# Moving top-k rounds, rotation copies, mask tiles and stores in a one-core encoder block

## The chip, the cores and the metric

The kernel runs on one core of one Trainium2 chip. The core has engines with queues of their own: PE (TensorE) multiplies matrices, DVE (VectorE) and ACT (ScalarE) work on tiles element by element, POOL (GpSimd) and SP (SyncE) here mostly issue DMAs. Each engine runs its instructions strictly in the order in which the program gives them. The metric is the device time of one execution in microseconds (us).

## What is computed

One layer of an encoder block on 512 frames of 2048 channels. A combined projection feeds a sparse attention (an index score picks 128 keys for each frame), a retention mixer with rotary positions, and two merge gates; then come output projections and a gated embedding. Cut to what matters here:

```python
h = rmsnorm(x, norm_gain)
proj = h @ w_in                       # split into 13 parts
# sparse attention, by chunks of 64 frames, topk = 128
index = einsum(relu(einsum(qi, ki)), w)
index = where(admissible, index, -inf)
_, sel = lax.top_k(index, topk)
bias = rel_table[t5_bucket(pos_sel - pos)]
logits = q @ k[sel] * scale + bias
a_out = softmax(logits) @ v[sel] * silu(az)
# retention, 8 heads
rq, rk = rope(rq, positions), rope(rk, positions) * R_KEY_DIM ** -0.5
scores = (rq @ rk) * intra_decay
y = scores @ rv + (rq * from_start) @ state
b_out = groupnorm(y) * silu(rz)
merged = sigmoid(ga) * (a_out @ w_a_out) + sigmoid(gb) * (b_out @ w_b_out)
r = x + merged @ w_o
out = rmsnorm(r + (p @ w_ple) * sigmoid(r @ w_ple_gate), final_gain)
```

## The kernel before

Everything is computed transposed: channels on the 128 partitions, 512 frames along the free dimension. Float32 weights are multiplied as two float16 parts. ACT rounds a tile of 128x1024 weights to its high part (`wh`, line 228), and DVE subtracts this from the weights to get the low part (`wl`, line 133). Both stand in rings of three tiles, so neither engine can run far ahead of PE. Units of weights are split three ahead (`AHEAD`) and loaded eight ahead.

Most of the projection is done in pairs of output blocks by `gemm_pair`, a seven-product scheme in 14 runs of 8 matmuls (112 matmuls). The products gather in the banks `ps_p`, `ps_v`, `ps_q`, `ps_r`. Four copies by ACT (`pv`, `e1`, `e2`, `e3`, line 341) and additions by DVE (`e_t`, line 345, and `go`, line 1212) make the two output blocks. A table, `SPLIT_AT`, says before which run which unit is split. DMAs that accumulate into a weight tile (line 193, POOL) and one addition by DVE (line 239) make the sums of weights that the scheme needs.

The order on each engine is written by hand. `step()` is called after every two matmuls of a pair (after three elsewhere) and counts ticks. `later(n, f)` runs `f` n ticks on. When nothing else is queued in `todo`, `step` takes one entry of the background queue `bg` every `state["rate"]` ticks. Behind the index scores, `bg` holds, in this order: sums of the normalized input, the top-k rounds, and the masks of the position bias.

A top-k round takes the eight largest entries of each row of a 128-row tile (`MAX8`) and then overwrites them (`MATCH_VALUE_LOAD` and `MATCH_REPLACE8`). There are 16 rounds for each of three tiles of 256, 384 and 512 columns, 48 in all. The last round of a tile writes the mask `mneg`, which attention adds to the bias. A mask of the bias is an ACT `Sign` over a row of positions (line 902). Four banks of masks at a time go through PE (`bias_mm`) and ACT to the DRAM tensor `scr`, from which attention loads its bias.

The stages in order of time: index queries and scores; the retention's values (`values`, twice) and the attention's values (`values_pair`); eight heads, each with one pair for the retention's query and key and two pairs for the merge gates; four pairs for `rz`, eight for the attention's queries and keys, four for `az`; attention beside `project_b`; the output projections; the embedding gate; the end.

At the end of a retention pair, `rotate` takes each of the two output blocks: two ACT copies that swap its halves (`rb`, lines 1012 and 1013), then two products and a sum on DVE (lines 1014 to 1016). The query scaling (`qt`, line 1023), the scores (`ps_rs`), the decay (`at`), the transposed keys (`kn`) and the states follow at fixed ticks, in the list `steps`.

ACT also issues DMAs: evicted values (`rd`), gates (`sgb`, `sga`, line 1222). Small tiles come from a pool of 28 general slots (`U`), larger ones from five big slots (`B`).

Of the kernel before, what the change touches and what calls it, by code (L numbers as in the profile page):

```python
# [17 lines left out]
OP = mybir.AluOpType  # L18
# [50 lines left out]
def block_kernel(tc, flag, cfg, xT, pT, posb, posq, w_in, w_v, w_r0, w_r1, w_ik, w_a, w_b, w_o, w_ple, w_gate,  # L69
# [7 lines left out]
    with contextlib.ExitStack() as ctx:  # L77
# [11 lines left out]
        def U(name, dt=F32):  # L89
            return up.tile([128, L], dt, name=name, tag="u")  # L90
# [226 lines left out]

        def gemm(ids, parts, name, c=ALL, order=None):
            return gemms([(ids, slice(0, 128), parts, c, name)], order=order)[0]

# [611 lines left out]

        rounds = [lambda r=r, t=t: topk_round(t, r == 15) for r in range(16) for t in range(1, NT)]
        bg.append(lambda: xn_load(0))
# [3 lines left out]
        bg.extend(rounds)  # L938
        bg.append(lambda: state.update(rate=BG_RATES[3]))
        banks = [(t, tuple(range(8 * t + g, 8 * t + g + n))) for t, n in reversed(tuple(enumerate((4, 2, 1, 1))))  # L940
                 for g in range(0, 8, n)]
        for n in range(0, len(banks), 4):
            run = banks[n:n + 4]
            bg.extend([lambda b=b, i=i, j=j: bias_mask(b, i, j > 1) for j, b in enumerate(run)
                       for i in range(4 * len(b[1]))])
            bg.append(lambda run=run: waiting.append(run))

        def split(src, name, lag=0, gain=None, checked=True):
# [49 lines left out]
        def retention(h):  # L998
# [10 lines left out]
            def rotate(i, o):  # L1009
                E[i] = o  # L1010
                b = U("rb")
                act.activation(b[0:64, :], o[64:128, :], AF.Copy)
                act.activation(b[64:128, :], o[0:64, :], AF.Copy)
                later(3, lambda: dve.tensor_mul(o, o, ct))
                later(5, lambda: dve.tensor_mul(b, b, st))
                later(7, lambda: dve.tensor_add(o, o, b))
                if i:
                    for n, f in steps:
                        later(n, f)
# [79 lines left out]

            steps = [(9, queries), (24, scores), (24, lambda: keys(0)), (28, decay), (29, lambda: keys(1))]  # L1100
            steps += [(n, lambda i=i: states(i)) for i, n in enumerate((39, 41, 43))]
            steps += [(51, lambda t=t: values_out(t)) for t in range(NT)]
# [12 lines left out]
        for i in range(2):  # L1115
            for t, ps in enumerate(values(u_rv[i], RV[i], x_load if i else lambda s: None)):
                later(3 * t, lambda i=i, t=t, ps=ps: act.dma_start(rd[i, t, :, 0:RV[i]], normal(ps, t, RV[i])))
        state["rate"] = BG_RATES[1]
# [83 lines left out]
        def hold(on):  # L1202
            state["hold"] = on

        def gate_pair(ids, finish):
            t = B("go")
            outs = [t[:, 0:512], t[:, 512:1024]]
            have = [0, 0]

            def done(c0, c1, i, q):  # L1210
                o = outs[i]
                dve.tensor_add(o[:, q], c0, c1)  # L1212
                have[i] += 1
                if have[i] == 2:
                    later(1, lambda: finish(i, o))

            gemm_pair(ids, Xh, done)

        def to(dst, func):
            def finish(i, o):  # L1220
                act.activation(o, o, func, scale=un_x)  # L1221
                act.dma_start(dst[i], o)
            return finish

        for h in range(NH):
            if state["rate"] == BG_RATES[2]:
                later(38, lambda: hold(True))
                later(64, lambda: hold(False))
            gate_pair(u_r[h], retention(h))
            for n in (2 * h, 2 * h + 1):  # L1230
                d, m = ((sgb, 2 * n), (sga, 2 * n - 16))[n >= 8]
                gate_pair(u_g[n], to(d[m:m + 2], AF.Sigmoid))
# [179 lines left out]
        for n in range(NH // 2):  # L1412
            if n == NH // 2 - 1:
                while bg or waiting:
                    bg.popleft()() if bg else bias_banks(waiting.popleft())
                for h in range(NH):
                    later(4 + 3 * h, lambda h=h: b_load(h))
                heads = [attention_head(h) for h in range(NH)]
                later(38, heads[0].pop(0)[1])
            gate_pair(u_az[n], to(zd[2 * n:2 * n + 2], AF.Silu))  # L1420
# [10 lines left out]
        for h in range(NH):  # L1431
            for n, f in heads[h]:
                later(max(n + HEAD * h + 10, 0), f)

# [110 lines left out]
        def finish_pair(n, s):  # L1545
# [30 lines left out]
            for i, f in zip(at, (mul, own, add, squares, lambda: gains(0), lambda: gains(1), sums)):  # L1576
                later(i, f)

        for m in range(ME):
            if m % 2 == 0:  # L1580
                later(8, lambda m=m: pw_load(m))
                s = B("go")
            pg = gemm(u_e[m], rparts, "ps_pg", order=R_ORDER if m == 0 else None)
            act.activation(half(s, m % 2), pg, AF.Sigmoid, scale=un_r)
            if m % 2:
                finish_pair(m // 2, s)
# [219 lines left out]
BG_RATE = 4  # L1806
BG_RATES = (2, 5, 40, 7, 5)
ADD_LAG = 24
X_BACK = (4, 6, 8, 10, 12, 14, 22, 24, 26, 28, 30, 32)
HEAD = 13  # L1810
WARM = 11
MANUAL = True
QK_LOW = 5, 9

# [102 lines left out]
```

## Time and profile before

| | |
|---|---|
| median of 3 runs | 1575.38 us (1575.31 to 1577.98) |
| profiled execution | 1577.83 us, of which the span is 1576.0 us |
| DVE, ACT, POOL busy | 83%, 60%, 14% of the span |
| mean granted clock of PE | 0.996 |

The page gives the busy time of each engine. The view of waits lists who waited for whom, with the total, the number and the longest in us. The table by stage cuts the time at given points. The timeline lists instructions in order of time, with the idle time before each and what ended it in brackets. A matmul's end is modelled, so neighbouring matmuls overlap in it and a short stop of PE may not show as idle time.

### The profile page before, as it was taken

Reading aid. Unit: us, or ns where it says so; the run is one execution under the profiler, and the core shown is the slowest. Engines: PE = TensorE matmul, PEld = TensorE weight load, DVE = VectorE, ACT = ScalarE, POOL = GpSimd, SP = SyncE. Lnnn points to the kernel's source line nnn. Section 1 sums busy time; section 2 is a strip of 40 time slices with the busy share of each in tenths; the row PEclk is TensorE's granted clock in tenths of the full one; section 3 lists DMA queues with packets and bytes.
Section 4 is the critical chain, followed back from the end, with each engine's and each line's share of the span. In section 5 each row is a group of like instructions: output and inputs, shape, how many; then the busy total and the mean of one; then the engine's idle time right before and its main releaser. Section 6 shows DMA issues by size and latency. Waiting matters only on the chain.

```text
span 1576.0 us, 25637 instructions
## 1 busy us (share of the span) xinstructions
PE 1549.7 (98%) x9321; PEld 893.4 (57%) x9321; DVE 1312.7 (83%) x2699; ACT 950.1 (60%) x1475; POOL 225.2 (14%) x254
## 2 busy tenths in 40 slices
PE   9999999999999999999999999999999999999996
PEld 5654445666665655566565566555544556545764
DVE  8899889989988988987777877786668888888875
ACT  7566545555555555676877776566644455576653
POOL 3100111111111111112332122100000111100101
PEclk9999999999999999999999999999999999999998
DMA  8436889789788889789999899998566799876973
GB/s 318 131 118 207 254 205 253 199 216 240 194 214 222 199 205 234 179 224 256 251 278 245 222 248 237 257 366 307 177 212 193 199 224 240 220 228 188 256 243 111
DMA packets 127882, 353.40 MB, mean 224 GB/s; under 512 B 15360, under 2 KB 28160, under 8 KB 127744
## 3 DMA queue, kind: packets, MB, share of 16 engines
q1 hardware_dynamic: 87280, 228.63, 42.9%
q0 software_dynamic: 27360, 98.06, 33.7%
q10 hardware_dynamic: 13104, 24.96, 4.3%
q8 instruction: 75, 1.23, 0.3%
q14 instruction: 63, 0.52, 0.1%
HBM read 308.60 MB, written 42.99 MB: 223 GB/s over the span
## 4 chain that ended last, share of the span: by engine, by line
PE 43%; DVE 4%; ACT 3%; issue 1%; ACTq 0%; DVEq 0%
PE ps_p L402 13%; PE ps_v L402 9%; PE ps_q L402 4%; PE ps_r L402 4%; PE ps_w L309 2%; PE ps_w L310 2%; PE ps_w L308 2%; DVE wl L133 1%; ACT bm L1319 1%; PE ps_pg L1667 1%; PE ps_pg L1669 1%; PE ps_pg L1668 1%; PE ps_pg L310 1%; ACT bm L1326 1%; DVE rl L133 1%
## 5 line engine op out<-in xcount | busy, mean ns | idle before, releaser
L133 DVE SCALAR_TENSOR_TENSOR wl<-wraw,wh 128x1024 f16<-128x1024 f32 (+3 forms) x472 | 565.0, 1208 | 123.2 <-ACT wh L228 120.0
L228 ACT ACTIVATE wh<-wraw 128x1024 f16<-128x1024 f32 (+3 forms) x471 | 483.8, 1038 | 225.3 <-DVE wraw L239 114.4
L402 PEld LDWEIGHTS <-wh 128*128 128x128 f16 x3008 | 293.6, 98 | 311.2 <-ACT wh L228 9.7
L402 PEld LDWEIGHTS <-wl 128*128 128x128 f16 x2912 | 283.3, 98 | 74.0 <-DVE wl L133 9.5
L193 POOL DMA_DIRECT2D wraw<-w_in x120 | 106.5, 966 | 545.5 <-DVE wl L133 342.6
L402 PE MATMUL ps_p<-hs,wh 128*128 128x512 f16 x640 | 151.2, 379 | 0.0
L341 ACT ACTIVATE e<-ps_p 128x512 f32<-128x512 f32 x152 | 89.8, 591 | 62.3 <-PE ps_p L402 57.0
L402 PE MATMUL ps_p<-hs,wl 128*128 128x256 f16 x640 | 83.1, 273 | 3.6 <-DVE wl L133 2.7
L402 PE MATMUL ps_r<-hs,wh 128*128 128x512 f16 x320 | 77.3, 385 | 5.9 <-ACT wh L228 5.9
L402 PE MATMUL ps_q<-ha,wh 128*128 128x512 f16 x320 | 75.7, 379 | 0.0
L402 PE MATMUL ps_p<-ha,wh 128*128 128x512 f16 x320 | 75.6, 379 | 0.0
L402 PE MATMUL ps_v<-hs,wh 128*128 128x512 f16 x320 | 75.6, 379 | 0.0
L402 PE MATMUL ps_v<-ha,wh 128*128 128x512 f16 x320 | 75.6, 379 | 0.0
L310 PEld LDWEIGHTS <-wl 128*128 128x128 f16 x460 | 45.0, 98 | 49.9 <-DVE wl L133 2.3
L1212 DVE TENSOR_TENSOR go<-e_t 128x256 f32<-128x256 f32 x160 | 68.2, 426 | 5.8
L308 PEld LDWEIGHTS <-wh 128*128 128x128 f16 x460 | 45.1, 98 | 44.3 <-ACT wh L228 0.5
L309 PEld LDWEIGHTS <-wh 128*128 128x128 f16 x460 | 45.0, 98 | 44.0
L193 POOL DMA_DIRECT2D wraw<-w_o x24 | 21.1, 941 | 327.8 <-DMA sm<-mbs 181.7
L902 ACT ACTIVATE mk<-relf,thr 128x512 f16<-128x512 f32 (+3 forms) x128 | 66.5, 554 | 1.6 <-ACT go L1221 1.6
L239 DVE TENSOR_TENSOR wraw<-wraw 128x1024 f32<-128x1024 f32 x52 | 63.7, 1225 | 1.8
L1221 ACT ACTIVATE go<-go 128x512 f32<-128x512 f32 x40 | 25.2, 631 | 64.3 <-DVE go L1212 64.3
L345 DVE TENSOR_TENSOR e_t<-ps_p,pv 128x512 f32<-128x512 f32 x48 | 33.1, 690 | 24.8 <-ACT e L341 24.7
(421 smaller groups left out, 2870.9 us busy)
## 6 DMA issues: line engine op xcount, KB each, us to landing
wraw<-w_in SPq DMA_DIRECT2D x170, 512.0 KB, 5.2
wraw<-w_in POOLq DMA_DIRECT2D x120, 512.0 KB, 8.0
wraw<-w_o SPq DMA_DIRECT2D x32, 512.0 KB, 5.5
wraw<-w_o POOLq DMA_DIRECT2D x24, 512.0 KB, 7.6
wraw<-w_gate SPq DMA_DIRECT2D x24, 512.0 KB, 5.2
wraw<-w_v SPq DMA_DIRECT2D x16, 512.0 KB, 6.8
wraw<-w_b SPq DMA_DIRECT2D x16, 512.0 KB, 6.2
wraw<-w_a SPq DMA_DIRECT2D x16, 512.0 KB, 4.1
```

The costliest lines, as they stand in the source:

```text
L133: dve.scalar_tensor_tensor(l, src, 1.0 if gain is None else gain, h, op0=OP.mult, op1=OP.subtract, **({"accum_out": column()} if checked a ...
L193: pool.dma_start(out=view(raw_tiles[r], nk, cols), in_=src[:, k0:k0 + nk, :], accum_op=OP.add)
L228: act.activation(h, raw, AF.Copy, scale=cfg.w)
L239: dve.tensor_add(raw, raw, view(raw_tiles[plus], nk, cols))
L308: pe.matmul(o, h[:, k, w], a, start=(s == order[0]), stop=False)
L309: pe.matmul(o, h[:, k, w], b, start=False, stop=False)
L310: pe.matmul(o, l[:, k, w], a, start=False, stop=(s == order[-1]))
L341: act.activation(E[n], src, AF.Copy)
L345: f(t, x, y)
L402: pe.matmul(o[:, co], w[:, k], src, start=(n < 4 and begin and k == 0 and j == 0), stop=(ended[n] == 16), skip_group_check=True)
L902: act.activation(bias_e[b][i // per][:, ln * (i % per):ln * (i % per + 1)], relf[:, :ln], AF.Sign, bias=thr[:, q:q + 1])
L1212: dve.tensor_add(o[:, q], c0, c1)
```

## The change

It applies to the kernel's fast variant, the one that runs here.

- Top-k: rounds that are left when the heads begin leave the background queue and are cut in two, `largest` (MAX8) and `remove` (the rest). In each head a half runs at ticks 15 and 44 and two at tick 106; in each pair behind the heads one at ticks 19 and 44. What is then left runs ahead of the last `az` pair. Masks start in the last head.
- `rotate`: for the second block the copies, products and sum come 8, 9, 11 and 13 ticks after the block is done, not 0, 3, 5 and 7. Scores, keys, decay and states follow four (states three) ticks later.
- Masks: all of them take general slots; two of four banks took big slots. Behind the heads one comes every sixth tick, not every fifth.
- Stores of values and gates by ACT are issued two ticks after the instruction that makes them.
- The splits of the first wide value weights, and of the second unit of the first embedding-gate weight, are asked for earlier.
- Attention heads start two ticks earlier.

```diff
+        def topk_halves(r, t):
+            a = R["isc"][:, IOFF[t]:IOFF[t] + 128 * (t + 1)]
+            m8 = []
+            def largest():
+                m8.append(S("m8", 8))
+                dve.max(m8[0], a)
+            def remove():
+                dve.match_replace(out=a, in_to_replace=m8[0], in_values=a, imm_value=-3.39e38)
+                if r == 15:
+                    dve.tensor_scalar(mneg[:, TOFF[t]:TOFF[t] + 128 * (t + 1)], a, -3.3e38, NEG,
+                                      op0=OP.is_gt, op1=OP.mult)
+            return largest, remove
...
+        n_behind = [-len(bg)]
+        if not fast:
+            bg.append(lambda: state.update(rate=BG_RATES[3]))
...
-            bg.extend([lambda b=b, i=i, j=j: bias_mask(b, i, j > 1) for j, b in enumerate(run)
+            bg.extend([lambda b=b, i=i, j=j: bias_mask(b, i, j > 1 and not fast) for j, b in enumerate(run)
...
+        n_behind[0] += len(bg)
...
             def rotate(i, o):
                 E[i] = o
-                b = U("rb")
-                act.activation(b[0:64, :], o[64:128, :], AF.Copy)
-                act.activation(b[64:128, :], o[0:64, :], AF.Copy)
-                later(3, lambda: dve.tensor_mul(o, o, ct))
-                later(5, lambda: dve.tensor_mul(b, b, st))
-                later(7, lambda: dve.tensor_add(o, o, b))
+                def swap():
+                    b = E["b"] = U("rb")
+                    act.activation(b[0:64, :], o[64:128, :], AF.Copy)
+                    act.activation(b[64:128, :], o[0:64, :], AF.Copy)
+                at = ROTATE_AT[i] if fast else ROTATE_AT[0]
+                later(at[0], swap)
+                later(at[1], lambda: dve.tensor_mul(o, o, ct))
+                later(at[2], lambda b=E: dve.tensor_mul(b["b"], b["b"], st))
+                later(at[3], lambda b=E: dve.tensor_add(o, o, b["b"]))
...
-            steps = [(9, queries), (24, scores), (24, lambda: keys(0)), (28, decay), (29, lambda: keys(1))]
-            steps += [(n, lambda i=i: states(i)) for i, n in enumerate((39, 41, 43))]
+            steps = [(9, queries), (28, scores), (28, lambda: keys(0)), (32, decay), (33, lambda: keys(1))]
+            steps += [(n, lambda i=i: states(i)) for i, n in enumerate((42, 44, 46))]
...
         for i in range(2):
-            for t, ps in enumerate(values(u_rv[i], RV[i], x_load if i else lambda s: None)):
-                later(3 * t, lambda i=i, t=t, ps=ps: act.dma_start(rd[i, t, :, 0:RV[i]], normal(ps, t, RV[i])))
+            def each(s, i=i):
+                if i:
+                    x_load(s)
+                    if fast and s == KT - 2:
+                        split_to(u_av[0][0] + AHEAD)
+            for t, ps in enumerate(values(u_rv[i], RV[i], each)):
+                def values_away(i=i, t=t, ps=ps):
+                    v = normal(ps, t, RV[i])
+                    later(2 if fast else 0, lambda: act.dma_start(rd[i, t, :, 0:RV[i]], v))
+                later(3 * t, values_away)
...
+        late_rounds = collections.deque()
+        def late_round():
+            if late_rounds:
+                late_rounds.popleft()()
         def gate_pair(ids, finish):
+            if state["banks"]:
+                for n in ROUNDS_AT:
+                    later(n, late_round)
...
                 act.activation(o, o, func, scale=un_x)
-                act.dma_start(dst[i], o)
+                later(2 if fast else 0, lambda: act.dma_start(dst[i], o))
...
+        if fast:
+            while len(bg) > n_behind[0]:
+                late_rounds.extend(halves[bg.popleft()])
+            state["rate"] = 1 << 30
         for h in range(NH):
+            if fast and h == NH - 1:
+                state["rate"] = BG_RATES[3]
...
+            if fast:
+                for n in ROUNDS_IN_HEAD:
+                    later(n, late_round)
...
+                todo.extend([late_round] * len(late_rounds))
...
-                later(max(n + HEAD * h + 10, 0), f)
+                later(max(n + HEAD * h + (8 if fast else 10), 0), f)
...
+        def split_second(s):
+            if s == 14:
+                split_to(u_e[0][1] + AHEAD)
...
-            pg = gemm(u_e[m], rparts, "ps_pg", order=R_ORDER if m == 0 else None)
+            pg = gemm(u_e[m], rparts, "ps_pg", order=R_ORDER if m == 0 else None,
+                      each=split_second if fast and m == 0 else None)
...
-BG_RATES = (2, 5, 40, 7, 5)
+BG_RATES = (2, 5, 40, 7, 6)
+ROTATE_AT = (0, 3, 5, 7), (8, 9, 11, 13)
+ROUNDS_AT = 19, 44
+ROUNDS_IN_HEAD = 15, 44, 106, 106
```

What it does to the order on the engines is shown at three places. First ACT where the retention pair of the sixth head ends and the next pair begins: `rb` are the copies of the rotation, `e` and `pv` copies of products, `wh` roundings. Before:

```order
L1012 ACTIVATE rb<-go 64x512
L1013 ACTIVATE rb<-go 64x512
L341 ACTIVATE e_6030<-ps_p 128x512
L228 ACTIVATE wh<-wraw 128x1024
L1012 ACTIVATE rb<-go 64x512
L1013 ACTIVATE rb<-go 64x512
L228 ACTIVATE wh<-wraw 128x1024
L341 ACTIVATE pv<-ps_v 128x512
```

And with the change:

```order
L1039 ACTIVATE rb<-go 64x512
L1040 ACTIVATE rb<-go 64x512
L341 ACTIVATE e_5997<-ps_p 128x512
L228 ACTIVATE wh<-wraw 128x1024 x2
L1039 ACTIVATE rb<-go 64x512
L1040 ACTIVATE rb<-go 64x512
L341 ACTIVATE pv<-ps_v 128x512
```

The second block's copies stand behind two roundings instead of one; the second of these is the one that feeds `ps_r`.

Then DVE at the same place: `go<-e_t` is the sum that ends the second block, `go<-go,ct` and the next two rows are its rotation, `qt` the scaled queries, `wl` low parts of weights. Before:

```order
L345 TENSOR_TENSOR e_t<-ps_r,e_6030 128x512
L1212 TENSOR_TENSOR go<-e_t 128x256
L133 SCALAR_TENSOR_TENSOR wl,stats<-wraw,wh 128x1024
L1014 TENSOR_TENSOR go<-go,ct 128x512
L1015 TENSOR_TENSOR rb<-rb,st 128x512
L1016 TENSOR_TENSOR go<-go,rb 128x512
L878 MAX m_6072<-isc 128x8
L879 MATCH_REPLACE isc<-m_6072,isc 128x384
L1023 TENSOR_TENSOR qt<-go,dect 128x384
L133 SCALAR_TENSOR_TENSOR wl,stats<-wraw,wh 128x1024 x2
L239 TENSOR_TENSOR wraw<-wraw 128x1024
```

And with the change, from a few rows earlier on:

```order
L942 MATCH_REPLACE isc<-m_5863,isc 128x384
L345 TENSOR_TENSOR e_t<-ps_v,e_5943 128x512
L1261 TENSOR_TENSOR go<-e_t 128x256
L133 SCALAR_TENSOR_TENSOR wl,stats<-wraw,wh 128x1024
...
L345 TENSOR_TENSOR e_t<-ps_r,e_5997 128x512
L1261 TENSOR_TENSOR go<-e_t 128x256
L133 SCALAR_TENSOR_TENSOR wl,stats<-wraw,wh 128x1024
L1044 TENSOR_TENSOR go<-go,ct 128x512
L1053 TENSOR_TENSOR qt<-go,dect 128x384
L1045 TENSOR_TENSOR rb<-rb,st 128x512
L133 SCALAR_TENSOR_TENSOR wl,stats<-wraw,wh 128x1024
L1046 TENSOR_TENSOR go<-go,rb 128x512
```

The round behind the rotation is gone, a `remove` half stands ahead of the additions, and the low parts stand between the steps of the rotation.

Last, ACT where the retention's values end and the attention's values begin: `rv` are evicted values, `rd` their stores, `wh<-wt` roundings of the wide value weights. Before:

```order
L418 ACTIVATE hs_2076<-t_2050 128x256
L418 ACTIVATE ha_2079<-xn 128x256
L991 ACTIVATE rv<-ps_vn,natx 128x496
L1117 DMA rd<-rv 128x496
L228 ACTIVATE wh<-wt 128x1024
L991 ACTIVATE rv<-ps_vn,natx 128x496
```

And with the change:

```order
L228 ACTIVATE wh<-wt 128x1024
L418 ACTIVATE hs_2080<-t_2050 128x256
L418 ACTIVATE ha_2083<-xn 128x256
L1016 ACTIVATE rv<-ps_vn,natx 128x496
L1155 DMA rd<-rv 128x496
L1016 ACTIVATE rv<-ps_vn,natx 128x496
```

A rounding that stood behind the first eviction and its store now stands ahead of both.

More of the change, by code (lines that the diff above doesn't have):

```diff
@@ L316, in block_kernel, with gemm @@
         ALL = slice(0, L)
-        def gemm(ids, parts, name, c=ALL, order=None):
-            return gemms([(ids, slice(0, 128), parts, c, name)], order=order)[0]
+        def gemm(ids, parts, name, c=ALL, order=None, each=None):
+            return gemms([(ids, slice(0, 128), parts, c, name)], order=order, each=each)[0]
         LO, HI = slice(0, 256), slice(256, 512)
@@ L931, in bias_banks @@
                 bias_out(b, ps)
-        rounds = [lambda r=r, t=t: topk_round(t, r == 15) for r in range(16) for t in range(1, NT)]
+        def topk_halves(r, t):
[10 more added lines that the diff above has]
+            return largest, remove
+        rounds = []
+        halves = {}
+        for r in range(16):
+            for t in range(1, NT):
+                f = lambda r=r, t=t: topk_round(t, r == 15)
+                halves[f] = topk_halves(r, t)
+                rounds.append(f)
         bg.append(lambda: xn_load(0))
@@ L938, in block_kernel @@
         bg.extend(rounds)
-        bg.append(lambda: state.update(rate=BG_RATES[3]))
+        n_behind = [-len(bg)]
+        if not fast:
+            bg.append(lambda: state.update(rate=BG_RATES[3]))
         banks = [(t, tuple(range(8 * t + g, 8 * t + g + n))) for t, n in reversed(tuple(enumerate((4, 2, 1, 1))))
```

## The prediction

> **What bounds the kernel now.** I read the page's busy line first, then the waits of PE, then a table by stage, and at last the timeline of the worst wait.
>
> ```profile
> span 1576.0 us, 25637 instructions
> PE 1549.7 (98%) x9321; PEld 893.4 (57%) x9321; DVE 1312.7 (83%) x2699; ACT 950.1 (60%) x1475; POOL 225.2 (14%) x254
> PE ps_r L402 <- ACT wh L228: 5.9, 6, 2.2
> PE ps_p L402 <- DVE wl L133: 2.7, 5, 0.9
> PE ps_vv L1190 <- DVE wl L133: 0.9, 1, 0.9
> PE ps_pg L310 <- DVE wl L133: 0.7, 1, 0.7
> PE ps_w L309 <- DVE al L133: 0.2, 1, 0.2
> ```
>
> PE issues matmuls nearly all the time, so no more can be gained than the places where it waits. What it waits for is always the same: a rounded weight, `wh` from ACT or `wl` from DVE, that came late. The waits show only part of the loss, because a matmul's end is modelled and covers short gaps. The loss itself is seen by cutting the trace at the eight heads of the retention and gate stage. Each head is three products of 112 matmuls plus the retention's own, so equal work. The columns are the window and its length, busy time and instruction count of PE, PEld, DVE, ACT and POOL, granted clock, DMA share, GB/s.
>
> ```profile
> 250.60:311.00 60.40, 59.20 (x368) 35.83 (x367) 57.47 (x117) 35.07 (x47) 11.43 (x13) 1.00 0.86 221
> 311.00:370.50 59.50, 58.87 (x369) 36.12 (x368) 54.30 (x107) 33.26 (x44) 10.40 (x11) 1.00 0.85 215
> 370.50:428.90 58.40, 58.40 (x368) 36.12 (x367) 53.67 (x107) 32.39 (x43) 8.99 (x10) 1.00 0.86 217
> 428.90:488.60 59.70, 58.88 (x369) 36.10 (x368) 53.83 (x106) 32.81 (x43) 9.18 (x11) 1.00 0.86 217
> 488.60:550.40 61.80, 59.16 (x369) 35.89 (x368) 54.53 (x107) 32.77 (x43) 10.53 (x11) 1.00 0.84 207
> 550.40:612.00 61.60, 59.03 (x368) 35.93 (x367) 53.68 (x107) 32.81 (x43) 9.91 (x11) 1.00 0.82 204
> 612.00:674.10 62.10, 59.88 (x368) 36.74 (x367) 53.89 (x103) 40.05 (x55) 9.41 (x11) 0.97 0.84 212
> 674.10:732.20 58.10, 58.10 (x368) 36.31 (x367) 49.13 (x94) 35.65 (x48) 9.92 (x10) 1.00 0.91 226
> ```
>
> The last head takes 58.10 us and PE never stops in it; it is the only one with no top-k round (94 DVE instructions against 103 to 117). The others take up to 62.10. The lengths add up to 481.60, which is 481.60 - 8 x 58.10 = **16.8 us over the floor**. That is the stage where the change can earn something.
>
> How a round does this is in the timeline at the end of a retention product (start, duration, engine, line).
>
> ```profile
> 572.11 1.05 ACT L228 ACTIVATE wh<-wraw 128x1024 f16<-128x1024 f32 x1
> 575.34 0.42 DVE L1212 TENSOR_TENSOR go<-e_t 128x256 f32<-128x256 f32 x1
> 575.80 0.63 ACT L1012 ACTIVATE rb<-go 64x512 f32<-64x512 f32 x1 [2.64 <-DVE go L1212]
> 576.44 0.63 ACT L1013 ACTIVATE rb<-go 64x512 f32<-64x512 f32 x1
> 577.09 1.06 ACT L228 ACTIVATE wh<-wraw 128x1024 f16<-128x1024 f32 x1
> 578.20 1.90 PE L402 MATMUL ps_r<-hs,wh 128*128 128x512 f16 x8 [1.99 <-ACT wh L228]
> 579.04 0.55 DVE L878 MAX8 m<-isc 128x8 f32<-128x384 f32 x1
> 579.70 0.54 DVE L879 MATCH_REPLACE8 isc<-m,isc 128x384 f32<-128x384 f32 x1
> ```
>
> DVE is behind. ACT stands 2.64 us at the rotation's copy `rb`, which needs DVE's `go`, and the rounding `wh` that PE wants is queued behind the two copies. PE waits 1.99 us.
>
> **The change part by part.** *Top-k rounds.* Their number and durations stay; 26 of the 48 are moved.
>
> ```profile
> 259.00:642.00 383.00, 14.54 (x26) 1.00 0.85 215
> L878 DVE MAX8 m<-isc 128x8 f32<-128x512 f32 x16 | 11.0, 690 | 0.0
> L879 DVE MATCH_REPLACE8 isc<-m,isc 128x512 f32<-128x512 f32 x16 | 10.8, 676 | 0.0
> L878 DVE MAX8 m<-isc 128x8 f32<-128x256 f32 x16 | 6.8, 423 | 0.0
> L879 DVE MATCH_REPLACE8 isc<-m,isc 128x256 f32<-128x256 f32 x16 | 6.5, 409 | 0.0
> L879 DVE MATCH_VALUE_LOAD isc<-m,isc 128x8 f32 x48 | 4.4, 92 | 1.6
> ```
>
> The first row counts MAX8 alone: 26 rounds in the first seven heads, 3.7 a head. A round is 690 + 92 + 676 = 1.46 us at its widest and 423 + 92 + 409 = 0.92 at its narrowest, 1.19 half-way. After the change each of the eight heads has four halves, which is two rounds or 2.4 us, and the other ten rounds stand in the ten products behind. DVE then has about 49.13 + 2.4 = 51.5 us of work in 58.1. The round that stood between the rotation and the next roundings at the end of the retention product is gone from there; one half (0.41 to 0.68 us, plus the value load) is put in ahead of that place instead.
>
> *Rotation copies behind a rounding.* In ACT's order the `wh` for `ps_r` comes ahead of the two copies. In the timeline above it could follow the `wh` of 572.11, that is, end near 574.3 if its weights are there, against the 576.2 at which PE wants it (578.20 - 1.99). So the `ps_r` waits go. What is late next is DVE: of the second copy's products, only one and the query scaling now stand ahead of `wl` for `ps_r`. With DVE as late as at 575.34 that `wl` would still come a good microsecond after PE wants it; the gain is whole only where DVE is less late, which is what fewer rounds are for.
>
> For both together I take what the third head shows. It had DVE work of 53.67 us, more than the 51.5 to come, and lost 58.40 - 58.10 = 0.3 us. Eight times 0.3 is 2.4 us left of 16.8, a gain of **14.4**. The bounds: all 16.8 goes, or half stays (8.4), since the rounds a head are about halved.
>
> A part of this loss is not waiting.
>
> ```profile
> 637.40:639.50 2.10, 0.00 (x0) 0.00 (x0) 1.91 (x4) 2.06 (x4) 0.00 (x0) 1.00 1.05 203
> 639.50:643.00 3.50, 3.46 (x9) 1.27 (x10) 3.40 (x8) 1.90 (x3) 0.00 (x0) 0.51 0.55 108
> ```
>
> Here PE stood for 2.10 us, and in the next 3.50 us the granted clock was 0.51: about 1.7 us more, in one of the two waits near 2 us. [...]
>
> *Splits and stores reordered.* The rounding for the wide value weights is asked for ahead of the evictions `rv` at the end of the retention values, and a second rounding of the first gate weight ahead of its sigmoid. These are the `ps_vv` and `ps_pg` waits above, 0.9 and 0.7 us: **1.6**, bounds 0 and 1.6. The stores that ACT issues two steps later cost the issue as before; ACT no longer stands for its own result.
>
> ```profile
> ACT wh L228 <- ACT go L1221: 6.5, 14, 0.7
> ```
>
> That is ACT's time, hidden behind PE except at late roundings; I count it at nothing, and if it shows, it is a gain of a few tenths. Attention starts two steps earlier, so the last head's `al` comes before PE asks: 0.2 us, bounds -0.5 and +0.5, since the steps of the heads now fall differently between the weight roundings.
>
> *Ten rounds and the masks behind the heads.*
>
> ```profile
> 732.20:805.00 72.80, 72.37 (x484) 42.27 (x483) 52.92 (x87) 60.96 (x90) 26.31 (x31) 1.00 1.00 270
> ```
>
> Here DVE is busy for 73% of the time. One round to a product of 18.2 us adds 1.19 us, 6.5%, which makes 79%; the last head ran at 49.13 of 58.10, 85%, without a wait. The window's idle PE time is 0.43 us. The masks here come at every sixth step instead of every fifth, so ACT, at 84% in this window, is eased; in the order of the program the last head gets 16 of them where it had 5. I take a **loss of 0.5**, bounds a gain of 0.4 (the idle time goes) and a loss of 3 (0.3 in each of the ten products).
>
> The last bias bank is now two products later, so its stores end later. The rows that say whether this is hidden:
>
> ```profile
> L927 POOL DMA_DIRECT2D scr<-bev x32: 531/538/869, 740.8 to 979.0; - x32
> L1282 SPq DMA_DIRECT2D bm<-scr x8: 319/320/365, 1027.2 to 1102.7; - x8
> DMA to landing us min/median/max: 3.5/6.3/8.9
> ```
>
> 979.0 + 2 x 18.2 + 8.9 = 1024.3, still ahead of the first load of the biases at 1027.2. It costs nothing; with that cover of 2.9 us gone, SyncE would stand at the load with the weights behind it.
>
> The sum, against the profiled execution's own 1577.83 us (span 1576.0 and 1.8 around it): 1577.83 - 14.4 - 1.6 - 0.2 + 0.5 = **1562.1**. The median of the three runs, 1575.38, is 2.45 lower. The matmuls are the same, so I take it that the median run simply has 2.45 us less of these waits, and that both come down to the same floor.
>
> **The rivals.** *Half stays*: DVE's lateness at the end of a retention product comes from the work there, not from the rounds, and the copies only change who is late. Then 8.4 us stay in the heads, and each later product loses 0.3: 1577.83 - 8.4 - 1.8 + 3 = 1570.6. For it: the `wl` reckoning above. Against: the last head had the old order of copies and lost nothing.
>
> *Late weights*: the waits come from transfers, and rounds only coincide with them; then next to nothing changes, about 1575.
>
> ```profile
> ACT wh L228 <- DMA wraw<-w_in: 11.9, 11, 2.2
> ```
>
> For it: eleven roundings waited for their weights, and the DMA share is 0.82 to 0.91 in the heads. Against: the last head moved the most, 226 GB/s, and did not wait, and the stage behind moves 270. [...]
>
> *Slower*: the halves stand where DVE has no room. The place is the half in front of the addition that feeds the rotation, and those at the same spots of the later products. If each of the 52 halves cost PE its own length, 0.6 us, that is 31 us, against the 18.6 that can be saved at most: 1577.83 - 18.6 + 31 = 1590. It decides from 0.36 us a half. Against: 26 whole rounds, placed without regard, cost 16.8 us, 0.32 a half, copies and all.
>
> **How the numbers follow.** The forecast, 1558 to 1567, gets 0.66; half stays 0.18; late weights 0.09; slower 0.07. A measurement of this kernel tells a difference of about 0.2%, 3 us, from none. Faster by more than that is the first two and a little of the third: 0.85; same 0.08; slower 0.07. The lower end takes all bounds at their best: 1577.83 - 16.8 - 1.6 - 0.5 - 0.4 = 1558.5, and up to 2 less if the median run's floor is lower than the profile's: 1556.5. The upper end is that of "half stays", 1571.
>
> **What would show it.** In the profile after: all eight heads within a few tenths of 58.1 us; no `ps_r` wait for `wh`; at the end of a retention product `wh` in ACT's timeline ahead of `rb`; no `ps_vv` and `ps_pg` wait; granted clock 1.00 in the seventh head. I am wrong if heads still take 60 us, if `wl` takes the place of `wh` in PE's waits, or if products behind the heads grow over 18.2 us (those with a bias bank excepted).

## The result, and the profile after

The changed kernel takes 1566.37 us (median of 4 runs, 1564.98 to 1567.84). The kernel before, run beside it, takes 1575.8 us (1575.31 to 1577.98). The ratio is 0.9938, with a 95% interval of 0.992 to 0.9955: faster by 0.6%. The forecast was 1562 us with a range of 1556.5 to 1571. The sign and the range held, and the gain is about two thirds of the one forecast. The profiled execution took 1566.16 us, close to the median.

The page of the profile after, its first lines:

```profile
span 1564.4 us, 25634 instructions
PE 1544.6 (99%) x9321; PEld 895.1 (57%) x9321; DVE 1308.9 (84%) x2699; ACT 949.6 (61%) x1475; POOL 227.0 (15%) x254
```

PE's busy share went from 98% to 99%. The work is the same, with 9321 matmuls as before. The view of PE's waits (total, number, longest, in us) tells what changed; the rest of it, three rows, was there before or is under 0.7 us:

```profile
PE ps_rs L1060 <- DVE go L1046: 2.3, 8, 0.3
PE ps_r L402 <- DVE wl L133: 2.1, 5, 0.8
...
```

The 5.9 us in which `ps_r` waited for `wh` from ACT are gone. In their place `ps_r` waits for `wl` from DVE, and the retention scores `ps_rs` wait for the rotated sum `go`, in all eight heads. So the rounding is no longer late, and DVE is. That is the sign which the prediction named as "I am wrong if".

The same eight heads as in the prediction, in a table of windows (length, busy time and count of PE, PEld, DVE, ACT, POOL, granted clock, DMA share, GB/s); first, fourth and last:

```profile
249.10:309.30 60.20, 59.01 (x368) 35.97 (x367) 56.49 (x114) 35.57 (x48) 12.08 (x13) 1.00 0.90 228
...
427.30:486.90 59.60, 58.50 (x369) 36.34 (x368) 51.29 (x100) 33.09 (x44) 9.98 (x10) 1.00 0.86 214
...
663.50:722.50 59.00, 58.48 (x368) 36.31 (x367) 51.63 (x100) 42.39 (x60) 9.91 (x10) 1.00 0.90 225
```

From the second head on DVE has between 51.2 and 52.0 us of work, about the 51.5 that were forecast, and the clock is full. Still no head comes down to 58.1 us, and the last one, which had 58.10 before, now has 59.0. The first is still over 60 us, which was another of the prediction's signs of being wrong.

Where the profiled difference comes from is read by cutting both traces at the same places of the program. Of before the heads and the attention:

```profile
250.62:732.21 481.59, 471.51 (x2937) 289.04 (x2936) 430.50 (x841) 274.80 (x365) 79.74 (x83) 1.00 0.86 215
...
1015.99:1236.31 220.32, 219.52 (x1151) 111.64 (x1150) 166.93 (x425) 118.00 (x249) 2.87 (x4) 1.00 0.74 248
```

And after: the heads, the products behind them, the attention, the rest.

```profile
249.09:722.49 473.40, 468.09 (x2937) 290.33 (x2936) 417.27 (x807) 276.33 (x365) 81.83 (x83) 1.00 0.87 219
722.49:1005.80 283.31, 283.19 (x1937) 169.33 (x1936) 230.38 (x414) 212.02 (x331) 73.49 (x93) 1.00 0.95 251
1005.80:1224.31 218.51, 218.50 (x1151) 111.70 (x1150) 166.49 (x425) 117.68 (x249) 3.12 (x5) 1.00 0.74 250
1224.31:1564.40 340.09, 326.88 (x2015) 197.18 (x2013) 277.43 (x571) 193.43 (x283) 36.34 (x41) 0.99 0.77 212
```

The heads lost 481.59 - 473.40 = 8.19 us, the attention 1.81, the stages ahead of the heads 1.53 (they end at 250.62 and at 249.09), the products behind 0.47 (283.78 before). The rest took 0.40 more. The heads are now 473.40 - 464.80 = **8.6 us** over the floor of 8 x 58.10, where the forecast was 2.4.

What makes DVE late is in the timeline where a retention product ends, here in the second head (start, duration, engine, line; in brackets the idle time before and what ended it):

```profile
326.14 0.68 DVE L942 MATCH_REPLACE8 isc<-m,isc 128x512 f32<-128x512 f32 x1
326.74 0.68 DVE L345 TENSOR_TENSOR e_t<-ps_v,e 128x512 f32<-128x512 f32 x1
...
332.93 0.42 DVE L1261 TENSOR_TENSOR go<-e_t 128x256 f32<-128x256 f32 x1
333.27 1.22 DVE L133 SCALAR_TENSOR_TENSOR wl<-wraw,wh 128x1024 f16<-128x1024 f32 x1
333.39 0.63 ACT L1039 ACTIVATE rb<-go 64x512 f32<-64x512 f32 x1 [1.69 <-DVE go L1261]
...
334.69 0.69 DVE L1044 TENSOR_TENSOR go<-go,ct 128x512 f32<-128x512 f32 x1 [0.19 <-ACT rb L1040]
335.30 0.55 DVE L1053 TENSOR_TENSOR qt<-go,dect 128x384 f32<-128x384 f32 x1
335.77 0.68 DVE L1045 TENSOR_TENSOR rb<-rb,st 128x512 f32<-128x512 f32 x1
336.37 1.22 DVE L133 SCALAR_TENSOR_TENSOR wl<-wraw,wh 128x1024 f16<-128x1024 f32 x1
337.51 0.69 DVE L1046 TENSOR_TENSOR go<-go,rb 128x512 f32<-128x512 f32 x1
337.65 0.39 PE L402 MATMUL ps_r<-hs,wl 128*128 128x256 f16 x2 [0.44 <-DVE wl L133]
338.35 0.91 PE L1060 MATMUL ps_rs<-go 128*128 128x128 f32 x6 [0.30 <-DVE go L1046]
```

From 326 to 338 us DVE works without a stop of more than 0.2 us. PE waits for the `wl` that begins at 336.37, and right after it for the sum of 337.51. Two explanations fit these lines. The half round of tick 44 (`MATCH_REPLACE8` at 326.14) pushes back all that follows. Or the new order of the rotation does it: `go*ct`, `qt` and `rb*st`, 0.69 + 0.55 + 0.68 us, stand ahead of the `wl`, and the sum is only just in time for the scores.

### The profile page after: what moved, and what is told of

Its sections match the earlier page's. It is cut to its first block, busy times and chain, and to the rows that moved or that the text cites. A ratio compares the mean times of both kernels' runs of the same rounds, so it can differ in the third digit from the quotient of the medians.

```text
span 1564.4 us, 25634 instructions
## 1 busy us (share of the span) xinstructions
PE 1544.6 (99%) x9321; PEld 895.1 (57%) x9321; DVE 1308.9 (84%) x2699; ACT 949.6 (61%) x1475; POOL 227.0 (15%) x254
```

## The experiments

Each kernel below differs from the changed one by the diff that is shown. The heads' length is from its profiled execution, with the cuts as above; the time is the median of all runs, and the ratio is to the kernel before, run on the same chip. A length of the heads is one execution's and varies by itself: "splits undone" has the same program in the heads as the changed kernel and took 1.8 us less there. Differences of the heads below about 2 us therefore decide nothing. Three of the profiled executions lie well off their kernel's median: "rounds only" 4.3 us above it, "before" 2.0 above, "old rotation, no rounds in the heads" 2.4 below.

| kernel | heads, us | time, us | ratio, 95% interval |
|---|---|---|---|
| before | 481.59 | 1575.8 | 1 |
| changed | 473.40 | 1566.37 | 0.9938 (0.992 to 0.9955) |
| rounds only | 480.05 | 1568.4 | 0.9956 (0.9943 to 0.997) |
| rotation only | 480.05 | 1573.6 | 0.9987 (0.9978 to 0.9996) |
| no rounds in the heads | 469.16 | 1561.95 | 0.9916 (0.9902 to 0.9929) |
| scores later | 477.19 | 1569.28 | 0.9965 (0.9951 to 0.9979) |
| half after the rotation | 467.93 | 1560.36 | 0.9902 (0.9888 to 0.9916) |
| old rotation, no rounds in the heads | 468.12 | 1562.58 | 0.9922 (0.9909 to 0.9935) |
| queries later, no rounds in the heads | 468.17 | 1560.21 | 0.9897 (0.9883 to 0.9912) |
| splits undone | 471.64 | 1565.59 | 0.9935 (0.9923 to 0.9947) |
| half after the rotation, queries later | 466.54 | 1559.41 | 0.9894 (0.9879 to 0.991) |
| two halves ahead | 477.60 | 1569.29 | 0.9957 (0.9941 to 0.9973) |
| old rotation, half after | 469.73 | 1562.12 | 0.991 (0.9894 to 0.9926) |
| scores later, halves away | 472.82 | 1566.0 | 0.995 (0.9936 to 0.9963) |

**One part alone: the rounds.**

```diff
-            steps = [(9, queries), (28, scores), (28, lambda: keys(0)), (32, decay), (33, lambda: keys(1))]
-            steps += [(n, lambda i=i: states(i)) for i, n in enumerate((42, 44, 46))]
+            steps = [(9, queries), (24, scores), (24, lambda: keys(0)), (28, decay), (29, lambda: keys(1))]
+            steps += [(n, lambda i=i: states(i)) for i, n in enumerate((39, 41, 43))]
-ROTATE_AT = (0, 3, 5, 7), (8, 9, 11, 13)
+ROTATE_AT = (0, 3, 5, 7), (0, 3, 5, 7)
```

> The rotation as before: both blocks at ticks 0, 3, 5, 7, scores at 24 as before; everything else as in the changed kernel. The eight heads took 481.6 us before and 473.4 after, over a floor of 8 x 58.1 = 464.8. Theory A (the rounds made DVE late, and moving them is the gain; the new order of the rotation costs): the heads come to 465 to 469 us, below the changed kernel, since the last head of before had this order, no round, and lost nothing; no wait of ps_rs for go. Theory B (the gain is the copies behind the rounding): the heads stay near 480, with the waits of ps_r for wh of before. In between, near 473 to 476, both parts are needed.

Its waits of PE:

```profile
PE ps_r L402 <- ACT wh L228: 11.0, 8, 2.4
```

The waits for `wh` are not only back, they are in all eight heads. The last head, which had lost nothing in the kernel before, stands there for 2.37 us: it had no round then, and now has four halves. So halves of rounds in a head make DVE late, the copies wait for DVE, and with the old order `wh` waits behind the copies: in the last head the first copy stands 2.03 us for `go` and starts at 692.26 us, the second starts at 692.90, the rounding that PE waits for at 694.19, and PE goes on at 695.28. The profiled execution was the slowest of this kernel's five (1572.67 us, median 1568.4), so theory B's 480 is met only at the dear end; by the medians the rounds alone save 7.4 us, most of what both parts save (9.4), and the intervals of the two ratios overlap. Some 1.7 us of the 480.05 went to a lower clock behind the wait in the last head (shown in the last section).

**One part alone: the rotation.**

```diff
-            while len(bg) > n_behind[0]:
-                late_rounds.extend(halves[bg.popleft()])
-            state["rate"] = 1 << 30
...
-            if fast and h == NH - 1:
-                state["rate"] = BG_RATES[3]
...
-ROUNDS_AT = 19, 44
-ROUNDS_IN_HEAD = 15, 44, 106, 106
+ROUNDS_AT = ()
+ROUNDS_IN_HEAD = ()
```

The change of rate behind the rounds is in the background queue again, as before.

> The top-k rounds whole and in the background queue as before, the rotation and all else as in the changed kernel. Theory A (rounds): the heads stay at 478 to 482 us, and PE waits for wl at ps_r and for go at ps_rs in place of wh. Theory B (copies): the heads are near 473.4, as in the changed kernel.

```profile
PE ps_r L402 <- DVE wl L133: 6.1, 5, 2.5
...
PE ps_rs L1059 <- DVE go L1045: 1.8, 6, 0.3
```

As theory A has it: 480.05 us. With the copies out of the way, PE waits as long for the next thing that DVE makes, 6.1 us for `wl` where it had been 5.9 for `wh`. The saving of 2.2 us in the medians is about what the attention alone saves (1.8 us in the profile of the changed kernel), and that is in this kernel too. The rotation by itself is worth next to nothing.

**No half in the heads.**

```diff
-ROUNDS_AT = 19, 44
-ROUNDS_IN_HEAD = 15, 44, 106, 106
+ROUNDS_AT = 10, 19, 36, 44
+ROUNDS_IN_HEAD = ()
```

> No half of a round in the heads; four halves instead of two in each product behind them, at ticks 10, 19, 36 and 44. Theory C (what is left in the heads, 8.6 us, comes from the halves that still stand there, the one ahead of the rotation above all): the heads come to 465 to 467. Theory D (it comes from the order of the rotation on DVE: three operations of 0.55 to 0.69 us ahead of the low part for ps_r, and the rotated sum only two ticks ahead of its use): the heads stay at 470 to 474 and ps_rs still waits about 0.46 us for go in each of them. In the products behind the heads, twice the rounds cost either nothing (they keep 18.2 us) or up to 0.3 us each.

The heads come to 469.16 us, between the two. Two of the waits that are left there, and the window of the products behind the heads, which now hold all the halves:

```profile
PE ps_rs L1060 <- DVE go L1046: 0.5, 2, 0.3
PE ps_r L402 <- DVE wl L133: 0.4, 1, 0.4
```

```profile
719.02:1002.16 283.14, 283.14 (x1937) 169.38 (x1936) 244.47 (x463) 212.13 (x331) 73.45 (x93) 1.00 0.95 251
```

The halves were half of what was left: 473.40 - 469.16 = 4.2 of 8.6 us. Behind the heads they cost nothing. DVE has 244.47 us of work there, against 230.38 in the changed kernel, and the window is 283.14 long, against 283.31.

**Scores later.**

```diff
-            steps = [(9, queries), (28, scores), (28, lambda: keys(0)), (32, decay), (33, lambda: keys(1))]
-            steps += [(n, lambda i=i: states(i)) for i, n in enumerate((42, 44, 46))]
-            steps += [(51, lambda t=t: values_out(t)) for t in range(NT)]
-            steps += [(57, norm), (70, scale), (90, lambda: back(0))]
+            steps = [(9, queries), (31, scores), (31, lambda: keys(0)), (35, decay), (36, lambda: keys(1))]
+            steps += [(n, lambda i=i: states(i)) for i, n in enumerate((45, 47, 49))]
+            steps += [(54, lambda t=t: values_out(t)) for t in range(NT)]
+            steps += [(60, norm), (72, scale), (90, lambda: back(0))]
```

> Scores, keys, decay, states, values and norm three ticks later (scores at 31), 1 us of PE's time; all else as in the changed kernel. Theory D (order): the waits of ps_rs for go, 0.46 us in seven heads and 0.32 in one, 3.5 us in all, go, and those of ps_r for wl stay: the heads come to 470 us. Theory C (DVE is late because of its work): what PE gains at the scores it loses at the next low part, and the heads stay at 473.

Neither: the heads take 477.19 us, longer than in the changed kernel. The waits of `ps_rs` did go, and a dearer one came. Its row, and the timeline in the second head:

```profile
PE ps_y L1097 <- DVE state L1086: 5.7, 8, 1.1
```

```profile
349.51 0.42 DVE L939 MAX8 m<-isc 128x8 f32<-128x256 f32 x1
...
350.05 0.41 DVE L942 MATCH_REPLACE8 isc<-m,isc 128x256 f32<-128x256 f32 x1
350.38 0.60 DVE L1086 SCALAR_TENSOR_TENSOR state<-state,ps_kv 128x128 f32<-128x128 f32 x2
...
350.71 0.49 PE L1097 MATMUL ps_y<-state,qt 128*128 128x128 f32 x2 [0.40 <-DVE state L1086]
```

Three ticks later, the update of `state` falls on the tick of the two halves at 106. They stand ahead of it, and the values `ps_y` wait for it. In the changed kernel the same two halves make no such wait: in its second head the update, at 345.85 us, is ahead of them, at 348.57. This reading is tested by the last experiment.

**One half moved.**

```diff
-ROUNDS_IN_HEAD = 15, 44, 106, 106
+ROUNDS_IN_HEAD = 15, 100, 106, 106
```

> The half at tick 44, ahead of the additions that feed the rotation, moved to tick 100; the halves at 15 and 106 and all else as in the changed kernel (heads 473.4 us; without any half 469.2). If the half at 44 alone makes the low part for ps_r late: the heads come to 469 to 470, and ps_r waits for wl no more. If it is the work of DVE in all: they stay at 473.

Its heads in one window, its largest wait in them, and the same place in its second head as in the timeline above:

```profile
249.53:717.46 467.93, 466.45 (x2937) 290.70 (x2936) 416.99 (x807) 276.50 (x365) 81.70 (x83) 1.00 0.88 221
```

```profile
PE ps_rs L1060 <- DVE go L1046: 0.6, 2, 0.3
```

```profile
325.11 0.68 DVE L345 TENSOR_TENSOR e_t<-ps_v,e 128x512 f32<-128x512 f32 x1
...
334.73 1.22 DVE L133 SCALAR_TENSOR_TENSOR wl<-wraw,wh 128x1024 f16<-128x1024 f32 x1
...
336.86 0.38 PE L402 MATMUL ps_r<-hs,wl 128*128 128x256 f16 x2
```

This is the answer. DVE does the same work in the heads, 416.99 us against 417.27, in as many instructions, and the heads are 473.40 - 467.93 = 5.5 us shorter. The addition `e_t` follows the low part at once, the low part for `ps_r` ends at 335.95, and PE takes it at 336.86 without a wait. Even the 469.16 us with no half at all is not better: the other three halves of a head show no cost where they stand. The mended order is worth 6 us of the time (1560.36 against 1566.37; the intervals of the ratios do not meet).

**The dose.**

```diff
-ROUNDS_IN_HEAD = 15, 44, 106, 106
+ROUNDS_IN_HEAD = 44, 44, 106, 106
```

> A dose: both halves of the first round of a head, at ticks 15 and 44, now at 44, ahead of the additions that feed the rotation; all else as in the changed kernel. None there gave heads of 467.9 us, one 473.4, which is 0.69 a half. If each half there costs PE its own length (0.41 to 0.69 us with 0.09 of the value load): 477 to 480. If DVE's lateness has a ceiling set by the rings of weights: 474 or less.

```profile
PE ps_r L402 <- DVE wl L133: 5.6, 7, 1.2
PE ps_rs L1060 <- DVE go L1046: 2.4, 8, 0.3
```

The heads take 467.93, 473.40 and 477.60 us with none, one and two halves ahead of the additions. The groups of the changed kernel's instructions give the lengths, over all the halves that were cut (busy time, mean in ns):

```profile
L939 DVE MAX8 m<-isc 128x8 f32<-128x256 f32 (+2 forms) x27 | 15.0, 555 | 0.0
L942 DVE MATCH_REPLACE8 isc<-m,isc 128x256 f32<-128x256 f32 (+2 forms) x27 | 14.7, 543 | 0.0
```

The half at 44 removes: 0.54 us and 0.09 for the value load, 8 x 0.63 = 5.1, measured 5.5. The half that the dose adds searches: 8 x 0.56 = 4.4, measured 4.2. Over the eight heads a half at this place costs PE about its own length. That is a mean: between the kernels with and without the half at 44, single heads differ by 0.2 to 1.2 us. So DVE has next to no slack there, though it is idle for 12% of the heads.

**The old rotation without halves in the heads, and with the half moved.** The rotation's diff of the first experiment, with the diff of the third, and with the diff of the fifth:

> The rotation as before the change and no half in the heads (four in each product behind). This completes the square of the two parts: heads 481.6 us with neither, 480.05 with either alone, 473.4 with both, 469.2 with the new rotation and no halves. If the old order is only bad where a round stands beside it, as the last head of before says (58.10 us, no round, old order): 8 x 58.1 and some 2 us at the entry of the first head, 467 us, with no wait of ps_r for wh. If the copies ahead of the rounding are late whatever DVE does: 474 or more, with ps_r waiting for wh a good half microsecond in each head.

> The rotation as before the change, the rounds in halves, with the half of tick 44 at tick 100. If the copies moved behind the rounding matter only when DVE is late: the heads are near 468, as with the old rotation and no halves (468.1). If the new order earns something of its own: it shows here as waits of ps_r for wh, 472 or more.

`ps_r`'s wait for `wh` in the first of them, and in the second:

```profile
PE ps_r L402 <- ACT wh L228: 1.8, 4, 0.9
```

```profile
PE ps_r L402 <- ACT wh L228: 3.0, 5, 1.3
```

468.12 and 469.73 us: with the rounds out of the way the old order loses little. With the new order the same two are 469.16 and 467.93. Without halves the order does not matter (1562.58 and 1561.95 us, overlapping intervals). With the half moved the new order seems some 1.8 us better, in the heads and in the time (1562.12 against 1560.36), but the intervals of these two overlap as well. By the medians both of these kernels with the old rotation are some 4 us faster than the changed one, though the intervals just overlap. So most of the gain does not hang on the new order.

**Queries later**, without halves in the heads, and with the half moved:

```diff
-            steps = [(9, queries), (28, scores), (28, lambda: keys(0)), (32, decay), (33, lambda: keys(1))]
+            steps = [(20, queries), (28, scores), (28, lambda: keys(0)), (32, decay), (33, lambda: keys(1))]
```

> The new rotation, no half in the heads (four in each product behind), and the query scaling at tick 20 instead of 9, so that 0.55 us less of DVE stands ahead of the low part for ps_r and of the rotated sum. With no halves the heads took 469.2 us, in which ps_rs still waited 0.17 to 0.47 us for the sum in six heads and ps_r 0.61 for wl in one, 2.3 in all. If the order on DVE makes them: they go, and the heads come to 467. If the sum waits for the two ACT copies instead: they stay, 469.

> Both mends together: the half of tick 44 at tick 100 (alone: heads 467.9 us, time 1560.36) and the query scaling at tick 20 (alone, with no halves: 468.2 and 1560.21). In the run with the half moved, PE still lost 1.75 us to the rotated sum and its low part. If that is DVE's order: the heads come to 466 and the time to 1558.5. If one mend already makes DVE early enough: 468 and 1560.

The first of the two kernels takes 468.17 us in the heads, between its two expectations and 1 us less than without the shift. That is within what the heads vary by, so it does not tell whether the sum waits for DVE's order or for the copies. Two heads of the second kernel, the third and the last:

```profile
368.04:426.09 58.05, 58.05 (x368) 36.41 (x367) 51.77 (x100) 33.15 (x44) 9.98 (x10) 1.00 0.88 222
...
658.71:716.76 58.05, 58.05 (x368) 36.41 (x367) 51.58 (x100) 42.36 (x60) 9.91 (x10) 1.00 0.90 228
```

Four of its eight heads are at 58.05 us and all but the first within 0.3 of it, and no wait for `go` or `wl` is left at the end of a retention product. The first head keeps 59.59. On DVE it still holds two whole rounds and work for the attention's values, and PE waits 0.57 us there for a `wl`, at 261.53 us. One half, at 258.51, stands ahead of that `wl`, but without any half the first head is no shorter (60.07 us in the kernel with the queries later); what makes it longer was not tried. With the half moved the query scaling seems worth 1.4 us in the heads, which is within what they vary by, and of the time it is within the error. The 1559.41 us are the best time here, 1.06% below before (0.9 to 1.21).

**The splits undone.**

```diff
-                    if fast and s == KT - 2:
-                        split_to(u_av[0][0] + AHEAD)
...
-                      each=split_second if fast and m == 0 else None)
+                      each=None)
```

> The two roundings asked for earlier (the wide value weights, the first embedding-gate weight) are asked for where they were; all else as in the changed kernel. If they are worth what the two waits of before say: ps_vv waits 0.9 us and ps_pg 0.7 again, 1.6 us more in those two stages, the heads unchanged at 473 to 474. If PE's waits only move: less than 0.5.

```profile
PE ps_pg L310 <- DVE wl L133: 0.6, 1, 0.6
```

`ps_pg` waits again, so that split takes a wait of 0.6 to 0.7 us away. That it shortens the stages behind the attention is not shown: they take 340.8 us here, 340.1 in the changed kernel, but 339.7 in the kernel before, which had the wait. `ps_vv` does not wait here. In the kernels that do ask early, whose program is the same up to there, it waited 0.9 (rotation only), 0.7, 0.5, 0.4, 0.2 and seven times not at all. That wait comes and goes by itself, and these runs do not show that the edit does anything for it. The time is the same as with the splits.

**Scores later, and the halves away.** The steps of the fourth experiment, and:

```diff
-ROUNDS_IN_HEAD = 15, 44, 106, 106
+ROUNDS_IN_HEAD = 15, 44, 130, 130
```

> Scores, keys, decay, states, values and norm three ticks later, as in the run that lost 5.7 us at ps_y, and the two halves of tick 106 at 130; the half at 44 stays where it is. If that loss came from the two halves, which fall on the tick of the state's update and stand ahead of it on DVE: the waits of ps_y for state go, and so do those of ps_rs, and the heads come to 470 us (473.4 less 3.5). If it came from the shift itself (the update behind one more low part): ps_y still waits for 4 us or more and the heads stay at 475 to 477.

```profile
PE ps_r L402 <- DVE wl L133: 3.4, 6, 0.8
...
PE ps_y L1097 <- DVE state L1086: 0.2, 1, 0.2
```

`ps_y` waits 0.2 us instead of 5.7, and `ps_rs` not at all: the two halves had made that loss. But the heads take 472.82 us, not 470. `ps_r` waits 3.4 us for `wl`, where it was 2.1 in the changed kernel, so part of what the scores no longer wait for is lost at `ps_r`; and the halves at 130 lengthen the products that they now stand in, by up to 0.55 us in five of the heads (18.75 where 18.2 is the floor). The sum of my expectation missed this price.

## Why the prediction was right or wrong

**The heads.** The mechanism held as far as DVE's lateness came from the rounds. That the copies have to go behind the rounding as well is not borne out: by the medians the rounds alone save 7.4 of 9.4 us, the rotation alone 2.2, and with the half moved the old rotation takes 1562.12 us, no more than the changed kernel. The step that failed is the size of what is left, "I take what the third head shows": 0.3 us a head. It was drawn from DVE's total work in a head, 53.67 us there and 51.5 to come. The total does not tell: the changed kernel and the one with the half moved have the same total and differ by 5.5 us. The part of the prediction on the rounds had the right fact, that one half of 0.41 to 0.68 us "is put in ahead of that place instead", and gave it no price. At its own length, 8 x 0.63 = 5.1, the heads' term would have been 14.4 - 5.1 = 9.3, against 8.2 measured.

**Half stays** came near the heads' number (8.4 us to stay, 8.6 measured) with the wrong reason; that is luck. It held that the lateness comes from the work at the end of the product and not from the rounds; taking one half away from there ends it. What it said of `wl` is right: it is what PE waits for next.

**Slower** named the place, "the half in front of the addition that feeds the rotation", and the price, a half's own length. Both are right for that half. It was wrong that all 52 would pay it: three of four in a head, and all that stand behind the heads, show no cost.

**Late weights** is out: the same transfers with one half moved lose 5.5 us less.

**Splits**, forecast 1.6: that the wait of `ps_pg`, 0.7, goes is shown, but not that time was gained by it; the 0.9 for `ps_vv` is not shown, since that wait varies by itself. **Attention**, forecast 0.2, measured 1.81, and in all thirteen changed kernels the stage took 218.46 to 218.76 us where it was 220.32. Of the waits, those of `ps_pt` for `bm` (0.5 us), of `ps_o` for `pt` (0.2) and of `ps_w` for `al` (0.2) are gone; the prediction names only the last. Which edit did it (the two ticks, the masks or the stores) was not tried. **Rounds and masks behind the heads**, forecast a loss of 0.5: a gain of 0.47, and all the halves fit there for nothing. The count was one short: 27 rounds were cut, not 26 (`x27` in the groups above), and eleven stand behind the heads, not ten. The row that I counted in began at 259 us; two more searches stand between the start of the heads and there. **Stores**: I wrote that ACT no longer stands for its own result. It does:

```profile
ACT wh L228 <- ACT go L1270: 6.9, 15, 0.7
```

Before it was 6.5 us in 14 places, so two ticks did not change it. No run takes the stores alone, so what they earn or cost is not shown.

Behind the attention nothing was gained (339.69 us before, 340.09 after) although the `ps_pg` wait went; what took its place was not followed. Of the forecast's error in the profiled execution, 1566.16 - 1562.1 = 4.1 us, the heads make 14.4 - 8.2 = 6.2. The attention, the products behind the heads and the stages ahead of them give 1.6, 1.0 and 0.6 back, and the rest, at +0.4 where -0.7 was forecast, takes 1.1. That so much came back is luck: the prediction gives no reason for the gain in the attention or behind the heads.

## What to carry to other kernels

Where an engine is a little late at one place in each pass of a loop, its busy share over the pass doesn't tell what a filler costs; its place does (here DVE worked 417.27 and 416.99 us in heads of 473.40 and 467.93 us). Look for the chain that ends last, and put fillers behind the link that this engine adds to it: here the 0.63 us of a removing half ahead of an addition cost 0.68 us a head on average, and the same half 56 ticks later showed no cost. And when a step is shifted by a fixed number of ticks, look at what else is due on the tick on which it lands (here two halves, and 5.7 us of waits for `state`).

## What was not expected of the hardware

In the prediction a gap of 2.10 us in PE's work was followed by a granted clock of 0.51. The kernel with the rounds only shows this once more, behind a wait of 2.37 us in the last head:

```profile
693.30:695.30 2.00, 0.02 (x1) 0.02 (x2) 1.78 (x5) 1.97 (x4) 0.00 (x0) 1.00 1.02 184
695.30:698.80 3.50, 3.50 (x14) 2.00 (x15) 2.91 (x5) 3.50 (x6) 0.00 (x0) 0.65 0.49 102
698.80:702.00 3.20, 3.20 (x27) 3.00 (x27) 2.44 (x5) 1.78 (x4) 0.00 (x0) 0.85 0.59 150
```

That is 3.50 x 0.35 + 3.20 x 0.15 = 1.7 us more, as in the prediction.

But the kernel with the rotation only has a longer one, 2.52 us, and keeps its clock:

```profile
639.00:641.50 2.50, 0.03 (x1) 0.00 (x0) 2.50 (x6) 0.04 (x1) 0.00 (x0) 1.00 0.32 62
641.50:645.00 3.50, 3.15 (x27) 2.74 (x28) 3.46 (x5) 0.39 (x1) 0.00 (x0) 1.00 0.45 150
```

So the length of the gap alone does not decide at this size: behind 2.10 us the clock went to 0.51, behind 2.37 us to 0.65 and then 0.85, and behind 2.52 us it stayed at 1.00. What tells the three gaps apart was not tried.
